# Moving token row factors, column sums and weight sums from TensorE and VectorE to memory and GpSimd in a one-core encoder layer

## The chip, the cores and the metric

The kernel runs on one core of one Trainium2 chip. The metric is the device time of one execution, in microseconds (us). The engines are named as in the profile: PE is TensorE, DVE is VectorE, ACT is ScalarE, POOL is GpSimd, SP is SyncE, which here issues all transfers.

## What is computed

One layer of a hybrid encoder on 4096 tokens of width 1024. The tokens are normalised, multiplied by one combined weight matrix, and split into attention operands (q, k, v), two gates (g_a, g_p) and a pooling branch u_p. Windowed attention and a multi-scale pooling are gated, concatenated, multiplied by an output matrix, normalised again and added to the input:

```
h = rmsnorm(x, pre_norm_g)
q, k, v, g_a, u_p, g_p = split(h @ w_in)
a = banded_attention(q, k, v, rel_bias, sink) * silu(g_a)
p = multiscale_pool(u_p, pool_w, pool_scale) * silu(g_p)
x = x + rmsnorm(concat(a, p) @ w_out, post_norm_g)
```

The input norm divides each token by the root of its mean square. That divisor is one number for each token, called the row factor below.

## The kernel before

**Two stages.** The first stage (up to about 495 us of the span) computes the three projections that need all channels of the pooling branch and the gates: GP (g_p), UU (u_p with the pooling matrices multiplied into its weights) and GA (g_a). The second stage does q, k, v, the attention and the output product, and is not touched.

**Numbers as pairs.** Every operand of a product is a pair of float16 tiles, high and low part, so that a product takes three matmuls. For token operands (tile `xb`, and `xt` for sums of token halves) ACT writes the high part and DVE then writes the low part as the difference (`b_low`, `t_low`, helper `tt`, L304). For weights (tile `wq`) ACT writes the high part (`w_high`, L557) and DVE the low part (`w_low`, helper `stt`, L307).

**Token groups.** The 4096 tokens are eight groups of 512, m = 0 to 7. Group 0 is multiplied plainly (`plain`, 192 matmuls for each of GP, UU, GA). Groups 1 to 7 use a Strassen-like scheme (`quad`) with seven products for each of the three projections; it needs sums of weight blocks S1 to S4 (`sum_weights`: four additions of 128x1024 float32 for each projection, then the pair for each sum) and sums of token blocks (`t_sums`: one addition of 512 and two of 256 columns). A product is issued in steps of six matmuls (one of four k blocks); in the profile the rows of L634 are these steps.

**Row factors.** For each group, ACT squares the token rows with a running sum, POOL takes the power -1/2 (`root`, tile `rs4`, one column for each 128 tokens), and PE spreads the 512 factors over all partitions by a product with the identity (`spread_all`, L413, four float32 matmuls that the profile shows as eight) into a PSUM tile `bc`. DVE then multiplies the group's token tile `nt` by gain and factor (`norm`, L307, eight instructions of 512 for a group) and makes the operands from it.

**Weight scales.** Before a weight becomes a pair it is scaled by a power of two from its largest column norm: ACT squares it into a bf16 tile `sq` (128x1024, `w_square`), PE adds the eight blocks of 128 columns and the partitions with eight matmuls against ones (`w_norm`, L528, tiles `n2ga`, `n2gb`, `n2a`, `n2u`, `n2b`), and DVE derives the scale (`w_scale`, from L188 on).

**What sets the order.** In the first stage each piece of work is a step with an engine, an estimated cost, a due time and its dependences (`do(...)`). A planner walks through these with the estimated costs, always taking the ready step with the lowest due time, and the instructions are then written out in that order. Each engine works its list strictly in order: an engine that comes to an instruction whose input isn't there waits, even if later ones could run. POOL's `tt` steps are costed with `pool(n)`, DVE's with `dve(n)`:

```
def dve(n):
    return 0.1 + n * 0.0012
def pool(n):
    return 0.15 + n * 0.0023
```

The planner knows nothing of one engine slowing another.

The helpers that record many operations have one line each: L304 is every two-tensor operation (`tt`), on DVE or POOL; L307 is every scalar-tensor-tensor on DVE (`stt`); L296 a tensor with a scalar.

Of the kernel before, what the change touches and what calls it, by code (L numbers as in the profile page):

```python
# [17 lines left out]
P = 128  # L18
S = 4096
D = 1024  # L20
KT = D // P
T = 512
NM = S // T
# [33 lines left out]
class Steps:  # L57
# [28 lines left out]
    def run(self):  # L86
        n_steps = len(self.steps)
        users = [[] for _ in range(n_steps)]
        open_deps = []
        for n, s in enumerate(self.steps):  # L90
            open_deps.append(len(s[5]))
            for d in s[5]:
                users[d].append(n)
        ready = [0.0] * n_steps
        begun = [None] * n_steps
        free = dict.fromkeys(("PE", "DVE", "ACT", "POOL", "SP"), 0.0)
# [38 lines left out]
def hybrid_layer(ctx: ExitStack, tc, io, out):  # L135
    nc = tc.nc
# [4 lines left out]
    dram = ctx.enter_context(tc.tile_pool(name="dram", bufs=1, space=DRAM))  # L141
# [8 lines left out]
    mhalf = const.tile([P, 1], F32, name="mhalf")  # L150
# [6 lines left out]
    sw = const.tile([P, 18], F32, name="sw")  # L157
# [5 lines left out]
    gs = const.tile([P, 1], F32, name="gs")  # L163
# [10 lines left out]
    epss = const.tile([P, 1], F32, name="epss")  # L174
    psc = const.tile([P, 4], F32, name="psc")

    f_row = dram.tile([NH, 512], F32, name="f_row")
    f_scr = dram.tile([NH, FR + 1, NF], F32, name="f_scr")
    x_scr = dram.tile([NU, P, 2, 2, HK, UT], F16, name="x_scr")
# [30 lines left out]
    with ExitStack() as actx:  # L210
        pa = actx.enter_context(tc.tile_pool(name="pa", bufs=1))
        psa = actx.enter_context(tc.tile_pool(name="psa", bufs=1, space=PSUM))

        GP, UU, GA = range(3)
# [6 lines left out]
        onesf = pa.tile([P, P], F32, name="onesf")  # L221
        edge = pa.tile([P, 4, 16], F32, name="edge")
        rs4 = pa.tile([P, 4], F32, name="rs4")
        xn1 = pa.tile([P, D], F32, name="xn")
# [4 lines left out]
        pw = ws[:, :T].rearrange("p (j c) -> p j c", j=4)  # L229
        turns = dict.fromkeys(("sq", "n2", "wup"), 0)  # L230

        def turn(name):
            turns[name] += 1
            return turns[name] % 2
# [68 lines left out]
        def tt(eng, out, in0, in1, op):  # L303
            eng.tensor_tensor(out=out, in0=in0, in1=in1, op=op)  # L304
# [210 lines left out]

        n2_t = {}

        def w_square(raw, z):
            A.activation(
                sqt[z].rearrange("p (g c) -> p g c", g=2) if len(raw.shape) == 3 else sqt[z], raw,  # L520
                AF.Square,
            )

        def w_norm(z, group, i, n, b):
            if i == 0:
                n2_t[group] = psa.tile([P, n, P], F32, name=f"n2{group}", tag=f"n2{b}")
            for k in range(KT):
                nc.tensor.matmul(  # L528
                    n2_t[group][:, i], ones16, sqt[z][:, k * P : (k + 1) * P], start=(k == 0),
                    stop=(k == KT - 1), skip_group_check=True,  # L530
                )

        def w_scale(group, cols):
# [4 lines left out]
        def w_gates(dst, cols):  # L538
            t_scalar(V, dst, isc[:, cols], 1.0 / H_SCALE, ALU.mult)

        def norms(keys, last, views, reads, group, cols):
            n, b = len(views), turn("n2")
            for i, (key, view, r) in enumerate(zip(keys, views, reads)):
                z = turn("sq")
                do("ACT", act(D), key, w_square, view, z, r=r, w=[f"sqt{z}"])
                do("PE", 0.5, key + 0.5, w_norm, z, group, i, n, b, r=["ones", f"sqt{z}"],
                   w=[f"n2{b}"])
# [29 lines left out]
        def sum_weights(q, scale, group, key, step, eng, again=False):  # L577
# [8 lines left out]
            if again:  # L586
# [11 lines left out]
            pair(q, S4, 1, scale, key + 3.5 * step, group)  # L598

        norms([5, 5], 5, [tile_view(GP, i) for i in (0, 1)], [tile_keys(GP, i) for i in (0, 1)],  # L600
              "ga", slice(0, 2))
        norms([13, 13], 13, [tile_view(GP, i) for i in (2, 3)], [tile_keys(GP, i) for i in (2, 3)],
              "gb", slice(2, 4))

        def gp_gates():
            w_gates(cg0, slice(0, 4))
# [67 lines left out]
                )  # L674


        cc = [pa.tile([P, 2, 2 * P], F32, name=f"cc{i}") for i in range(5)]
        cc_n = [0]

        def ccs(n):  # L680
# [219 lines left out]
        for j in range(4):  # L900
            ld(9.5 + 0.1 * j, wut[:, j], io["w_uT"][j], 0.5, w=[f"wut{j}"])
            z = turn("sq")
            for half in range(2):
                t = U0 + 4 * j + 2 * half
                do("PE", 1.0, t, u_prod, j, half, r=["ws", f"wut{j}"], w=[f"wup{half}"] + bcs)
                do("ACT", act(512), t + 1.2, u_square, j, half, z, r=[f"wup{half}"], w=[f"sqt{z}"])
                do("ACT", act(512), t + 1.2, u_keep, j, half, r=[f"wup{half}"],
                   w=[f"tile{UU}.{j}{half}"])
            do("PE", 0.5, U0 + 4 * j + 5, w_norm, z, "u4", j, 4, b, r=["ones", f"sqt{z}"],
               w=[f"n2{b}"])  # L910
# [16 lines left out]
        plain(GA, M0 + SL * 8 + 2)  # L927
        plain(UU, M0 + SL * 16 + 8)
        sum_weights(GP, com, "gc", M1 - 16, 3.0, "DVE", True)
        sum_weights(UU, sw[:, 8:9], "u4", M1 + 8, 3.0, "DVE")  # L930
        sum_weights(GA, sw[:, 4:5], "a4", M1 + 27, 3.0, "DVE")

        def prepare(m):
            key = start(m) - 55
            b = m % 2
            for i in range(4):
                xn, k = (xn1, "xn") if m > 1 or i % 2 == 0 else (NT[:, 2 * D : 3 * D], "ts")
                t = key - 9 + 3 * i if m > 1 else 20 + i
                ld(t - 3, xn, x_blk[BPM * m + i], 0.5, w=[k])
                do("ACT", 1.3, t, square, m, i, xn, w=[k, f"ssq{m % 2}.{i}"])  # L940
            do("POOL", 1.0, key + 3, root, m, slice(0, 4), r=[f"ssq{m % 2}.{i}" for i in range(4)] + ["mhalf"],
               w=["rs4", "rs0", "rs1"])
            do("PE", 1.2, key + 5, spread_all, m, r=["rs4", "ident"], w=[f"wup{m % 2}"])
            for c in range(HK):
                k = key + 14 + 9 * c
                n = f"n1.{c % 2}"
                ld(k - 9, n_view(m, c), xT[c][:, :, m], 0.5,
                   w=[n] + ([f"xsq{i}" for i in range(HK)] if m == 1 and c < 2 else []))
                for h in range(2):
                    do("DVE", dve(512), k + h, norm, m, c, h, r=["gs", f"wup{m % 2}"], w=[n])  # L950
# [1144 lines left out]
```

## Time and profile before

| | |
|---|---|
| median of 3 runs | 1174.7 us (1174.52 to 1175.09) |
| the profiled execution, its own time | 1174.91 us |
| its span, first to last instruction | 1172.8 us |
| PE busy | 1149.0 us, 98% of the span |
| PE weight loads busy | 883.4 us, 75% |
| DVE busy | 930.8 us, 79% |
| ACT busy | 702.6 us, 60% |
| POOL busy | 309.3 us, 26% |
| granted TensorE clock | 0.999 |

Rows of a timeline give the start in us from the span's beginning, the length of the merged piece in us, the engine, the line, the operation, output and inputs, and how many instructions are merged; a bracket at the end gives the idle time before it and what ended it. A PE row ends with the latency of its last matmul, which overlaps the next row, so the time that a piece takes from PE is the distance from its start to the next row's start. Rows of a source view give the least, median and greatest duration in ns.

### The profile page before, as it was taken

The page shows a single profiled execution, that of the slowest core. Times are in us where ns is not written, and L with a number is a line of the kernel's source. Part 1 is how long each engine was busy: PE and PEld are TensorE (multiplying, and loading weights), DVE is VectorE, ACT ScalarE, POOL GpSimd, SP SyncE. Part 2 cuts the span into 40 slices and gives each one's busy share as a digit, 9 for nine tenths or more (in the row PEclk, how much of TensorE's full clock was granted, in tenths as well). Part 3 has the DMA queues.
Part 4 walks back from the last instruction along what each step waited for, and adds up shares of the span by engine and source line. Part 5 has one row for each costly group of instructions (what it writes and reads, how often), then busy time and mean ns, then how long its engine had stood idle before and what let it go on. Part 6 is the DMA issues. An engine that isn't in the chain of part 4 may idle for free.

```text
span 1172.8 us, 33945 instructions
## 1 busy us (share of the span) xinstructions
PE 1149.0 (98%) x14304; PEld 883.4 (75%) x14304; DVE 930.8 (79%) x1865; ACT 702.6 (60%) x1459; POOL 309.3 (26%) x310
## 2 busy tenths in 40 slices
PE   5999999999999999999999999999999999999997
PEld 4998888888888888986667667576676667767653
DVE  6889997868788984558878878877887787887787
ACT  5875565546655552256676666666667666666672
POOL 0002111101101100201434434433533443443331
PEclk9999999999999999999999999999999999999999
DMA  8645488666756565299976886786777678687695
GB/s 315 218 111 169 162 261 268 185 234 221 255 189 232 153 186 176 56 279 209 263 184 140 191 198 133 197 196 159 182 193 185 142 190 200 136 194 160 164 234 144
DMA packets 292441, 224.65 MB, mean 192 GB/s; under 512 B 210704, under 2 KB 251920, under 8 KB 287680
## 3 DMA queue, kind: packets, MB, share of 16 engines
q1 hardware_dynamic: 292288, 222.48, 69.8%
q8 instruction: 112, 1.84, 0.6%
q14 instruction: 41, 0.34, 0.1%
HBM read 113.37 MB, written 60.33 MB: 148 GB/s over the span
## 4 chain that ended last, share of the span: by engine, by line
PE 50%; DVE 1%; ACT 0%; issue 0%; DVEq 0%; POOLq 0%; ACTq 0%
PE ms L1588 13%; PE aq L1227 12%; PE m L1588 9%; PE s L1272 4%; PE kv L1373 3%; PE o L1438 3%; PE kv L1227 3%; PE p L1438 2%; PE z L1560 1%; PE s L1560 0%; DVE pn L1336 0%; DVE mo L1627 0%; DVE p L1295 0%; ACT pn L1328 0%; DVE xt L1649 0%
## 5 line engine op out<-in xcount | busy, mean ns | idle before, releaser
L634 PEld LDWEIGHTS <-wq 128*128 128x128 f16 x4104 | 401.5, 98 | 52.7 <-issue 2.8
L634 PE MATMUL y<-xt,wq 128*128 128x256 f16 x1512 | 204.2, 273 | 0.9 <-ACT cc L742 0.9
L1306 ACT ACTIVATE p<-p,nm 128x385 f32<-128x385 f32 (+1 forms) x256 | 152.8, 599 | 35.0 <-POOL p L1289 20.3
L1227 PE MATMUL aq<-xb,xb 128*128 128x256 f16 x1024 | 173.4, 273 | 0.1
L1588 PE MATMUL ms<-wo,ys 128*128 128x512 f16 x720 | 162.7, 379 | 0.1
L1336 DVE SCALAR_TENSOR_TENSOR pn<-p,rd,pn 128x384 f16<-128x384 f32 (+1 forms) x256 | 156.1, 660 | 6.8 <-ACT pn L1328 6.8
L1295 DVE CUSTOM_DVE_ANT_0 p<-s,nt,nsink 128x384 f32<-128x384 f32 (+1 forms) x256 | 155.9, 665 | 1.8 <-PE s L1272 1.7
L1227 PEld LDWEIGHTS <-xb 128*128 128x128 f16 x1280 | 125.1, 98 | 22.8 <-issue 6.6
L1227 PE MATMUL aq<-xb,xt 128*128 128x256 f16 x512 | 139.6, 273 | 0.1
L1328 ACT ACTIVATE pn<-p,rd 128x384 f16<-128x384 f32 (+1 forms) x256 | 134.4, 596 | 4.2 <-issue 1.1
L1588 PEld LDWEIGHTS <-ys 128*128 128x128 f16 x720 | 69.2, 98 | 81.4 <-issue 2.8
L304 POOL TENSOR_TENSOR yt<-yt,sg 128x512 f32<-128x512 f32 (+2 forms) x32 | 48.0, 1499 | 311.4 <-DVE yt L307 293.1
L1588 PE MATMUL m<-wo,y 128*128 128x512 f16 x540 | 121.8, 379 | 0.0
L1588 PEld LDWEIGHTS <-y 128*128 128x128 f16 x540 | 51.5, 98 | 62.9 <-issue 2.9
L1622 POOL TENSOR_TENSOR mo<-mo,gpost 128x512 f32<-128x512 f32 x39 | 63.8, 1635 | 94.7 <-ACT jkb L1611 93.5
L634 PE MATMUL plain<-xb,wq 128*128 128x256 f16 x576 | 68.8, 276 | 3.0 <-ACT xb L446 1.8
L1227 PEld LDWEIGHTS <-xt 128*128 128x128 f16 x640 | 62.6, 98 | 8.3
L634 PE MATMUL y<-xb,wq 128*128 128x256 f16 x504 | 68.8, 273 | 0.0
L634 PE MATMUL v<-xb,wq 128*128 128x256 f16 x504 | 68.6, 273 | 0.2 <-DVE cc L304 0.2
L634 PE MATMUL v<-xt,wq 128*128 128x256 f16 x504 | 68.6, 273 | 0.0
L634 PE MATMUL x<-xb,wq 128*128 128x256 f16 x504 | 68.3, 273 | 0.0
L1272 PE MATMUL s<-k_all,q 64*32 64x288 f16 (+7 forms) x3648 | 62.5, 266 | 1.3 <-issue 1.3
(212 smaller groups left out, 1907.8 us busy)
## 6 DMA issues: line engine op xcount, KB each, us to landing
nt<-in_xT SPq DMA_DIRECT2D x28, 512.0 KB, 4.7
x_scr<-xb SPq DMA_DIRECT2D x14, 1024.0 KB, 7.2
xb<-x_scr SPq DMA_DIRECT2D x14, 1024.0 KB, 7.3
xr<-in_x SPq DMA_DIRECT2D x28, 512.0 KB, 4.6
out<-xr SPq DMA_DIRECT2D x28, 512.0 KB, 2.6
xn<-in_x SPq DMA_DIRECT2D x27, 512.0 KB, 4.4
ga_scr<-cc SPq DMA_DIRECT2D x64, 128.0 KB, 2.1
raw<-in_w_out SPq DMA_DIRECT2D x16, 512.0 KB, 5.4
```

Source lines behind the costliest of these rows:

```text
L304: eng.tensor_tensor(out=out, in0=in0, in1=in1, op=op)
L634: nc.tensor.matmul(b[:, s], wq[:, slot[q, op], wv, s, k, :], x[:, xv, k, :], start=(first and k + s + wv + xv == 0), stop=(last and k == H ...
L1227: nc.tensor.matmul(acc, w[:, j, k, :], x[:, kh, v, kt, :], start=(n == 0), stop=(n == 3 * KT - 1),)
L1272: nc.tensor.matmul(s_ps[qs, gg, c0:c1], q_t[u, half][a, qi, jj, tl + 32 * hq : tl + 32 * hq + 32], k_all[a, ki, kc + c0 - s0 : kc + c1 - s ...
L1295: nc.vector.tensor_tensor_reduce(out=p_t[b, half][:, hh, :nk], in0=s_t[jj][:, gg, :nk], in1=bias[:, h, lo : lo + nk], scale=negc[:, h : h ...
L1306: nc.scalar.activation(p[:, hh, : nk + 1], p[:, hh, : nk + 1], AF.Exp, bias=nm_t[b, half][:, hh : hh + 1], scale=-1.0, accum_out=den_t[b, ...
L1328: nc.scalar.activation(prob_view(b, half)[:, 0, i], p_t[b, half][:, i, :nk], AF.Copy, scale=rd_t[b, half][:, i : i + 1],)
L1336: nc.vector.scalar_tensor_tensor(out=pn4[:, 1, i], in0=p_t[b, half][:, i, :nk], scalar=rd_t[b, half][:, i : i + 1], in1=pn4[:, 0, i], op0= ...
L1373: nc.tensor.matmul(av[:, i], x[:, kh, v, kt, i * P : (i + 1) * P], w[:, B_V, k, :], start=(n == 0), stop=(n == 3 * KT - 1),)
L1438: nc.tensor.matmul(o_t[b][side][a, half], v_t[ku][ks, vi, kt, a], pt[b, half][ks, pi, g, :, kb - kbs[0], (LOW, TOP)[side]], start=start, s ...
L1588: nc.tensor.matmul(z_t[u, tag], y[:, k, yi, :], wo[o][:, wi, k, :], start=(n == 0 and acc is None), stop=(n == 3 * HK - 1), skip_group_che ...
L1622: eng.tensor_tensor(out=mo, in0=mo, in1=gpost[:, cs], op=ALU.mult)
```

## The change

**Row factors of groups 3 to 7.** `spread_all` on PE stays for groups 1 and 2. For the others POOL's `rs4` is written to a scratch in memory (`rows_store`, 512 single float32 elements), and read back as one row broadcast to 128 partitions (`rows_load`, 256 KB) into a new SBUF tile `rows`, which `norm` reads in place of the PSUM tile. The token squares and `root` of these groups get due times 16 us earlier. In the plan a made-up engine "NET" stands for 12 us and 7 us of transfer time; it issues nothing.

**Column sums folded.** For six of the weight squares (two of GA's four, three of UU's four, and the one of the v weights) POOL first adds the tile's eight blocks in three steps of 512, 256 and 128 columns (`w_fold`), and PE then needs one matmul in place of eight. GA's four squares get tiles of their own (the `cc` tiles, not yet in use then), in place of taking turns in two.

**Weight sums.** The four additions of UU and the four of GA move from DVE to POOL; GP's stay on DVE.

```diff
+        def rows_store(m):
+            nc.sync.dma_start(rs_scr[m].rearrange("(i p) -> p i", i=4), rs4)
+
+        def rows_load(m):
+            bc[m] = rows
+            nc.sync.dma_start(
+                rows, rs_scr[m].rearrange("(o t) -> o t", o=1).to_broadcast([P, T])
+            )
...
+        def w_fold(z):
+            for n in (512, 256, 128):
+                tt(G, sqt[z][:, :n], sqt[z][:, :n], sqt[z][:, n : 2 * n], ALU.add)
+
-        def w_norm(z, group, i, n, b):
+        def w_norm(z, group, i, n, b, folded):
...
-            for k in range(KT):
+            last = 1 if folded else KT
+            for k in range(last):
...
+        def norm_step(z, key, group, i, n, b, folded):
+            if folded:
+                do("POOL", 3.2, key, w_fold, z, w=[sq_key(z)])
+            do("PE", 0.1 if folded else 0.5, key, w_norm, z, group, i, n, b, folded,
+               r=["ones", sq_key(z)], w=[f"n2{b}"])
...
-                z = turn("sq")
+                z = turn("sq") if len(views) < 4 else 2 + i
...
+                norm_step(z, key + 0.5, group, i, n, b, folded and i < 2)
...
+            norm_step(z, U0 + 4 * j + 5, "u4", j, 4, b, j < 3)
...
-        sum_weights(UU, sw[:, 8:9], "u4", M1 + 8, 3.0, "DVE")
-        sum_weights(GA, sw[:, 4:5], "a4", M1 + 27, 3.0, "DVE")
+        sum_weights(UU, sw[:, 8:9], "u4", M1 + 8, 3.0, "POOL")
+        sum_weights(GA, sw[:, 4:5], "a4", M1 + 27, 3.0, "POOL")
+
+        MS = 3
...
-            do("PE", 1.2, key + 5, spread_all, m, r=["rs4", "ident"], w=[f"wup{m % 2}"])
+            if m < MS:
+                spread_key = f"wup{m % 2}"
+                do("PE", 1.2, key + 5, spread_all, m, r=["rs4", "ident"], w=[spread_key])
+            else:
+                spread_key = "rsp"
+                do("SP", 0.6, key - 12, rows_store, m, r=["rs4"], w=["rs_scr"])
+                do("NET", 12.0, key - 12, lambda: None, w=["rs_scr"])
+                do("SP", 0.45, key - 8, rows_load, m, r=["rs_scr"], w=["rsp"])
+                do("NET", 7.0, key - 8, lambda: None, w=["rsp"])
```

The changed costs make the planner write out a new order for the whole first stage. On PE the list has 89 rows fewer: five spreads, and 42 matmuls against ones with their weight loads. Three places matter below.

POOL, from its second `root` to the gates of the first token group, before (`rs` are row factors, `ssq` the sums of token squares, `yt` the gated pooling output):

```order
L296 TENSOR_SCALAR ssq_117<-ssq_117 128x2
L304 TENSOR_TENSOR rs_113<-ssq_117,mhalf 128x2
L296 TENSOR_SCALAR ssq_118<-ssq_118 128x4
L304 TENSOR_TENSOR rs_113<-ssq_118,mhalf 128x4
L304 TENSOR_TENSOR yt_119<-yt_119,sg 128x504
```

The same engine and stretch now, its middle part (`cc` and `sq` hold weight squares that are folded, `raw` is GA's weights, `wq` here UU's):

```order
L308 TENSOR_TENSOR cc_125<-cc_125 128x512
L308 TENSOR_TENSOR cc_125<-cc_125 128x256
L308 TENSOR_TENSOR cc_125<-cc_125 128x128
L308 TENSOR_TENSOR sq_118<-sq_118 128x512
L308 TENSOR_TENSOR sq_118<-sq_118 128x256
L308 TENSOR_TENSOR sq_118<-sq_118 128x128
L308 TENSOR_TENSOR raw<-raw 128x1024
L300 TENSOR_SCALAR ssq_120<-ssq_120 128x4
L308 TENSOR_TENSOR rs_114<-ssq_120,mhalf 128x4
...
L308 TENSOR_TENSOR raw<-raw 128x1024 x3
L308 TENSOR_TENSOR wq<-wq 128x1024 x4
L308 TENSOR_TENSOR yt_121<-yt_121,sg 128x504
```

Between these two rows of `root` and the first gate stood nothing on POOL; now fifteen folding additions and eight weight sums stand around the second of them.

DVE, while it makes the operands of token group 1, before (`nt` alone is a token sum, `nt<-nt,gsc,bc` a norm, `xb` and `xt` are low parts, `wq<-wq` a weight sum of UU, `wq<-wq,sw` the low part of a weight pair):

```order
L307 SCALAR_TENSOR_TENSOR wq<-wq,sw 128x1024 x2
L304 TENSOR_TENSOR nt<-nt 128x512
L304 TENSOR_TENSOR nt<-nt 128x256 x2
L304 TENSOR_TENSOR xb_68<-nt,xb_68 128x2x2x256
L304 TENSOR_TENSOR wq<-wq 128x1024
L304 TENSOR_TENSOR xt_105<-nt,xt_105 128x4x256
L307 SCALAR_TENSOR_TENSOR nt<-nt,gsc,bc_799 128x512
L304 TENSOR_TENSOR wq<-wq 128x1024
L307 SCALAR_TENSOR_TENSOR nt<-nt,gsc,bc_799 128x512
L304 TENSOR_TENSOR wq<-wq 128x1024
L304 TENSOR_TENSOR nt<-nt 128x512
```

The same place now, from the last pair of UU's plain weights on:

```order
L311 SCALAR_TENSOR_TENSOR wq<-wq,sw 128x1024 x2
L311 SCALAR_TENSOR_TENSOR nt<-nt,gsc,bc_791 128x512
L311 SCALAR_TENSOR_TENSOR wq<-raw,sw,wq 128x1024
L308 TENSOR_TENSOR nt<-nt 128x512
L308 TENSOR_TENSOR nt<-nt 128x256 x2
L308 TENSOR_TENSOR xb_68<-nt,xb_68 128x2x2x256
L311 SCALAR_TENSOR_TENSOR nt<-nt,gsc,bc_791 128x512
L308 TENSOR_TENSOR xt_106<-nt,xt_106 128x4x256
L311 SCALAR_TENSOR_TENSOR nt<-nt,gsc,bc_791 128x512
L311 SCALAR_TENSOR_TENSOR wq<-wq,sw 128x1024
L308 TENSOR_TENSOR nt<-nt 128x512
```

The three sums have gone from between the token work, and low parts of later weight sums have moved up into their place.

PE, at the first folded square of GA (`n2a` is the column norm, `wup` a product for UU's weights, `plain` a product of group 0):

```order
L908 MATMUL wup_0_455<-ws,xt_67 128x128 x4
L549 LDWEIGHTS ones_71
L549 MATMUL n2a_465<-cc_124,ones_71 128x128
L660 LDWEIGHTS wq
L660 MATMUL plain_447<-xb_66,wq 128x256
```

Here stood eight matmuls against ones; the one that is left comes 24 matmuls of group 0 and one `wup` product later in PE's list than the first of the eight did, and needs the fold on POOL.

More of the change, by code (lines that the diff above doesn't have):

```diff
@@ L95, in run @@
         begun = [None] * n_steps
-        free = dict.fromkeys(("PE", "DVE", "ACT", "POOL", "SP"), 0.0)
+        free = dict.fromkeys(("PE", "DVE", "ACT", "POOL", "SP", "NET"), 0.0)
         dma_free = 0.0
@@ L223, in hybrid_layer @@
         rs4 = pa.tile([P, 4], F32, name="rs4")
+        rows = pa.tile([P, T], F32, name="rows")
         xn1 = pa.tile([P, D], F32, name="xn")
@@ L229, in hybrid_layer @@
         pw = ws[:, :T].rearrange("p (j c) -> p j c", j=4)
+        cc = [pa.tile([P, 2, 2 * P], F32, name=f"cc{i}") for i in range(5)]
+        sqt += [t.rearrange("p s c -> p (s c)").bitcast(BF16) for t in cc[:4]]
         turns = dict.fromkeys(("sq", "n2", "wup"), 0)
@@ L516, in hybrid_layer, with sq_key @@
         n2_t = {}
+        def sq_key(z):
+            return f"sqt{z}" if z < 2 else f"cc{z - 2}"
         def w_square(raw, z):
@@ L539, in w_gates, with norms @@
             t_scalar(V, dst, isc[:, cols], 1.0 / H_SCALE, ALU.mult)
-        def norms(keys, last, views, reads, group, cols):
+        def norm_step(z, key, group, i, n, b, folded):
[3 more added lines that the diff above has]
+               r=["ones", sq_key(z)], w=[f"n2{b}"])
+        def norms(keys, last, views, reads, group, cols, folded=True):
             n, b = len(views), turn("n2")
             for i, (key, view, r) in enumerate(zip(keys, views, reads)):
-                z = turn("sq")
-                do("ACT", act(D), key, w_square, view, z, r=r, w=[f"sqt{z}"])
-                do("PE", 0.5, key + 0.5, w_norm, z, group, i, n, b, r=["ones", f"sqt{z}"],
-                   w=[f"n2{b}"])
+                z = turn("sq") if len(views) < 4 else 2 + i
+                do("ACT", act(D), key, w_square, view, z, r=r, w=[sq_key(z)])
+                norm_step(z, key + 0.5, group, i, n, b, folded and i < 2)
             do("DVE", 1.5, last, w_scale, group, cols, r=["gs"], w=[f"n2{b}", f"sw{group}"])
@@ L674, in ga_out @@
                 )
-        cc = [pa.tile([P, 2, 2 * P], F32, name=f"cc{i}") for i in range(5)]
         cc_n = [0]
@@ L937, in prepare @@
                 xn, k = (xn1, "xn") if m > 1 or i % 2 == 0 else (NT[:, 2 * D : 3 * D], "ts")
-                t = key - 9 + 3 * i if m > 1 else 20 + i
+                t = key - 9 - early + 3 * i if m > 1 else 20 + i
                 ld(t - 3, xn, x_blk[BPM * m + i], 0.5, w=[k])
                 do("ACT", 1.3, t, square, m, i, xn, w=[k, f"ssq{m % 2}.{i}"])
-            do("POOL", 1.0, key + 3, root, m, slice(0, 4), r=[f"ssq{m % 2}.{i}" for i in range(4)] + ["mhalf"],
+            do("POOL", 1.0, key + 3 - early, root, m, slice(0, 4), r=[f"ssq{m % 2}.{i}" for i in range(4)] + ["mhalf"],
                w=["rs4", "rs0", "rs1"])
-            do("PE", 1.2, key + 5, spread_all, m, r=["rs4", "ident"], w=[f"wup{m % 2}"])
+            if m < MS:
[7 more added lines that the diff above has]
+                do("NET", 7.0, key - 8, lambda: None, w=["rsp"])
             for c in range(HK):
@@ L949, in prepare @@
                 for h in range(2):
-                    do("DVE", dve(512), k + h, norm, m, c, h, r=["gs", f"wup{m % 2}"], w=[n])
+                    do("DVE", dve(512), k + h, norm, m, c, h, r=["gs", spread_key], w=[n])
                 x_operands(m, c, k + 2, "DVE")
```

12 lines of the change are left out of this document (6 added, 6 removed).

## The prediction

> **What bounds the kernel now.** I read the page first, then PE's waits, then the timelines of PE, DVE and POOL at the places where the order changes.
>
> ```profile
> span 1172.8 us, 33945 instructions
> PE 1149.0 (98%) x14304; PEld 883.4 (75%) x14304; DVE 930.8 (79%) x1865; ACT 702.6 (60%) x1459; POOL 309.3 (26%) x310
> ```
>
> PE is busy for all but 23.8 us of the span. PE's waits, longest first, say where the rest is:
>
> ```profile
> PE sp L370 <- DMA ident<-in_ident: 7.0, 1, 7.0
> ...
> PE y L634 <- ACT cc L742: 0.9, 1, 0.9
> ```
>
> The large one is the first load. In the rest of the first stage, after the start, PE waits 0.9 us at most at a time. So each us taken from PE's list is a us of the span, as long as its inputs still come in time; and each new wait of PE is a us lost. The prices of what is taken away are in PE's timeline at group 1's spread (start, us, instructions):
>
> ```profile
> 61.48 3.44 PE L634 MATMUL plain<-xb,wq 128*128 128x256 f16 x30
> 64.75 1.06 PE L413 MATMUL bc<-ident,rs 128*128 128x128 f32 x8
> 65.64 0.82 PE L634 MATMUL plain<-xb,wq 128*128 128x256 f16 x6
> 66.30 0.61 PE L528 MATMUL n2u<-sq,ones 128*128 128x128 bf16 x8
> 66.75 27.67 PE L634 MATMUL plain<-xb,wq 128*128 128x256 f16 x252
> ...
> 151.70 1.16 PE L413 MATMUL bc<-ident,rs 128*128 128x128 f32 x8 [0.33 <-POOL rs L304]
> ```
>
> From start to start, a spread takes 65.64 - 64.75 = 0.89 us, eight matmuls against ones 0.45 us or 0.056 each, a product matmul 3.27 / 30 = 0.109 us.
>
> **What the change takes from PE.** Five spreads: 5 x 0.89 = 4.45 us. The wait of 0.33 us in front of group 3's spread goes with it. Six foldings leave one matmul of eight: 42 x 0.056 = 2.35 us. Together 7.1 us. If nothing else happened, 1174.9 would become 1167.8 for the profiled execution; the median lies 0.2 below that execution, so 1167.6.
>
> **What it puts on POOL, and what that does to DVE.** The two engines are not independent. Timelines of DVE (first fence) and POOL (second), with one gate near 145 us and one near 102 us:
>
> ```profile
> 101.95 1.22 DVE L304 TENSOR_TENSOR xt<-nt,xt 128x1024 f16<-128x1024 f32 x1
> 103.09 2.27 DVE L307 SCALAR_TENSOR_TENSOR wq<-wq,sw 128x1024 f16<-128x1024 f32 x1
> ...
> 144.78 0.74 DVE L307 SCALAR_TENSOR_TENSOR nt<-nt,gsc,bc 128x512 f32<-128x512 f32 x1
> 145.44 1.39 DVE L304 TENSOR_TENSOR yt<-ubuf 128x527 f32<-128x527 f32 x1
> ```
>
> ```profile
> 102.11 2.16 POOL L304 TENSOR_TENSOR yt<-yt,sg 128x504 f32<-128x504 f32 x1 [2.60 <-DVE yt L307]
> ...
> 144.99 1.27 POOL L304 TENSOR_TENSOR yt<-yt,sg 128x512 f32<-128x512 f32 x1 [20.31 <-DVE yt L307]
> ```
>
> At 144.99 POOL starts a product of two SBUF tiles. The norm on DVE, whose second tensor is in PSUM, takes its usual 0.74. The next DVE operation reads two SBUF tiles and takes 1.39 in place of 0.70 (row at 99.67 below): it stands until POOL is done at about 146.2. At 102.11 it is POOL's turn to stand, until DVE's 1.22 us operation ends at 103.1; then POOL goes first, and DVE's next takes 2.27. So operations with two SBUF tensors shut each other out for their whole length, and take turns.
>
> How long are POOL's new operations? Rows by line, and by length for the smallest (busy, mean ns):
>
> ```profile
> L304 POOL TENSOR_TENSOR yt<-yt,sg x32: 1263/1280/2181, 96.2 to 496.2; 128x512 f32<-128x512 f32 x24, 128x504 f32<-128x504 f32 x4, 128x520 f32<-128x520 f32 x4
> L1494 POOL TENSOR_TENSOR y<-yf,y x30: 1152/1155/1281, 518.8 to 1119.3; 128x512 f16<-128x512 f32 x30
> L1289 POOL COPY p<-nsink 128x4 f32<-128x4 f32 x64 | 18.0, 296 | 0.1
> ```
>
> A weight sum has 1024 float32 columns: 2.25 us on the line through 4 and 512 columns, 2.55 at twice 512; I take 2.4. In a sentence of its own: the Trainium skill (GPSIMD Engine Reference, section 3.1) gives 4497 ns for 2048 float32 columns, an estimate of 2.25 us for 1024, by which the four sums below would hold DVE 0.6 us less in all. A fold in 16 bits: 1.15 + 0.72 + 0.51 (same line, 256 and 128 columns) = 2.4 us, between 2.0 (the halves at proportional cost) and 3.5 (three times the first).
>
> *At the start, 33 to 43 us.* ACT's squares, DVE's GP sums and low parts, PE:
>
> ```profile
> 31.68 2.00 ACT L519 ACTIVATE sq<-raw 128x1024 bf16<-128x1024 f32 x2
> ...
> ```
>
> ```profile
> 33.63 2.47 DVE L304 TENSOR_TENSOR wq<-wq 128x1024 f32<-128x1024 f32 x2
> 36.02 0.69 DVE L304 TENSOR_TENSOR xb<-xb,xb 128x512 f16<-128x512 f32 x1
> 36.62 2.48 DVE L304 TENSOR_TENSOR wq<-wq 128x1024 f32<-128x1024 f32 x2
> ...
> 40.87 0.72 DVE L296 TENSOR_SCALAR wq<-wq,rat 128x2048 f16<-128x2048 f16 x1
> ```
>
> ```profile
> 26.30 6.72 PE L634 MATMUL plain<-xb,wq 128*128 128x256 f16 x60
> ...
> 36.38 1.06 PE L883 MATMUL wup<-ws,xt 128*128 128x128 f32 x8
> 37.27 0.61 PE L528 MATMUL n2a<-sq,ones 128*128 128x128 bf16 x8
> ```
>
> The first square is there at 32.7. POOL's 512 columns run from 32.9 to 34.05, then DVE's first sum (1.2) to 35.25, POOL's 256 to 35.97, the second sum to 37.17, POOL's 128 to 37.7. In the new list 84 product matmuls and one `wup` (37.27 - 36.38 = 0.89) stand ahead of the single matmul: PE comes to it at 26.30 + 84 x 0.109 + 0.89 = 36.4 and waits 1.3. The second fold starts behind `xb` (0.60, 36.62 - 36.02) at 38.3 and, with a sum (1.2) and a rescale (0.65) between its steps, ends at 42.5; PE is there 30 matmuls after the first, 37.7 + 0.06 + 3.27 = 41.0, and waits 1.5. Each change of turn is about 0.13 cheaper than these additions (145.44 + 1.39 is 0.13 before 144.99 + 1.27 + 0.70); with that off at each of the ten changes the waits are 0.8 and 0.7. Between 2.8 and 1.5 I take 2.0; 0 if POOL is not held up between its steps, 3.5 if each fold costs its upper bound. The UU folds near 50 to 63 us fall where DVE waits for ACT, and PE reaches their matmuls 0.5 to 3 us after they end by the same reckoning: I take 0.
>
> *At group 1, 65 to 101 us.* This is the large term. DVE's work from the first norm to the last low part of `xb`, and PE's use of it:
>
> ```profile
> 65.84 1.41 DVE L307 SCALAR_TENSOR_TENSOR nt<-nt,gsc,bc 128x512 f32<-128x512 f32 x2 [3.02 <-PE bc L413]
> ...
> 70.30 1.60 DVE L304 TENSOR_TENSOR nt<-nt 128x512 f32<-128x512 f32 x3
> 71.82 2.48 DVE L307 SCALAR_TENSOR_TENSOR wq<-wq,sw 128x1024 f16<-128x1024 f32 x2
> 74.22 1.22 DVE L304 TENSOR_TENSOR xb<-nt,xb 128x1024 f16<-128x1024 f32 x1
> 76.49 2.48 DVE L307 SCALAR_TENSOR_TENSOR wq<-wq,sw 128x1024 f16<-128x1024 f32 x2
> ...
> 91.91 1.23 DVE L304 TENSOR_TENSOR xt<-nt,xt 128x1024 f16<-128x1024 f32 x1 [1.12 <-ACT xt L464]
> ...
> 94.52 0.71 DVE L304 TENSOR_TENSOR ws<-ubuf 128x527 f32<-128x527 f32 x1 [0.73 <-ACT ubuf L718]
> ...
> 96.07 2.54 DVE L304 TENSOR_TENSOR nt<-nt 128x512 f32<-128x512 f32 x3
> 98.53 1.22 DVE L304 TENSOR_TENSOR xb<-nt,xb 128x1024 f16<-128x1024 f32 x1
> 99.67 0.70 DVE L304 TENSOR_TENSOR yt<-ubuf 128x527 f32<-128x527 f32 x1
> ```
>
> ```profile
> 99.49 0.91 PE L634 MATMUL y<-xb,wq 128*128 128x256 f16 x6
> ```
>
> DVE has only 1.12 and 0.73 us idle in 34 us, and its low part ends at 98.53 + 1.22 = 99.75. PE's step that reads it starts at 99.49, reads the low part with its third matmul, and is 0.09 longer than the others: PE meets DVE with no margin at all.
>
> Now the same stretch in the new lists. The norm of group 1 starts 65.84 + 12 x 0.109 - 35 x 0.056 = 65.2 (12 product matmuls more, 35 against ones fewer ahead of it). To the end of the low part DVE needs 33.9 (65.84 to 99.75), less three UU sums (1.2 each, from 33.63 to 36.02), plus three low parts moved up (1.2 each, from 71.82 to 74.22), plus the second pooling step (101.95 - 99.67 = 2.3), plus that step's gate on POOL (2.54 against 1.60: 0.9), less the idle 1.85: 35.3, so 100.5. PE comes to the step with 24 product matmuls and group 2's spread more, 35 matmuls fewer ahead: 99.7 + 2.6 + 0.9 - 2.0 = 101.2. Without the weight sums, no wait.
>
> With them: UU's four start on POOL when the last low part of UU's plain weights is done, near 78.3 (76.49 + 2 x 1.2, less the 0.6 by which the norm starts earlier), in the middle of DVE's full stretch. Under the first a norm fits (0.66, 145.44 - 144.78), so DVE loses about 1.6; the next three stand each between two DVE operations on SBUF tiles (a low part and the three of `nt<-nt`) and cost 2.4 - 0.13 = 2.27 each. With 0.3 from the last of GA's sums, which mostly fall while DVE waits for the spread and the scale, that is 8.7. The low part ends at 109.2; PE waits 8.0. The start's 2.0 shifts both and drops out. Bounds: 5.5 (three norms fall under the sums) to 12 (2.55 each, two of GA's sums on full stretches too).
>
> **Sum.** -7.1 + 2.0 + 8.0 = +2.9: 1174.9 becomes 1177.8 for a profiled execution, 1177.6 as a median. Behind 101 us DVE has its three low parts and one more sum done, so I expect no further wait.
>
> **What I cost at nothing.** The rows from memory:
>
> ```profile
> yf<-yp_scr SPq DMA_DIRECT2D x32, 256.0 KB, 3.9
> yp_scr<-yt SPq DMA_DIRECT2D x28, 4.0 KB, 1.6
> ```
>
> Store and load at these prices take 5.5 us; the plan leaves 19 (the NET steps of 12 and 7 in the diff). A group's 21 products of 24 matmuls take PE 55 us, so group 3 starts near 205 us, some 50 us after its spread now, and that hides it. SP's list has stores and loads behind the `rows_store`, which waits for POOL's `root`: up to 2 us late each, with tiles loaded further ahead than that. `norm` then reads two SBUF tiles, 0.70 in place of 0.74 us at best, but waits for gates; no PE step depends on it that closely. If the cover is gone it costs its own delay, up to 3 us.
>
> **The rivals.** *1. PE's gain comes through* (faster). The turns on POOL do not lengthen DVE's stretch, because the sums fall elsewhere or POOL's operations slip into DVE's idle time. For it: POOL's eight sums are 19 us in a stretch of 45, and DVE sheds eight of its own. It decides below 0.7 us of loss on DVE; the break-even is 0.7 + 7.1 - 2.0 = 5.8 us. Price: -7.1 + 0 to 2: 1168 to 1170. Against it: the rows at 103.09 and 145.44. In a sentence of its own: the Trainium skill (SBUF — State Buffer, Who interferes with whom) says that a GpSimd read and a DVE instruction with two SBUF inputs shut each other out for the whole instruction, against this change, and the rows here agree (1.39 for 0.70). *2. Half of it* (about equal): norms under the sums, waits of 4 to 5 us: 1173 to 1175.5. *3. Memory as the wait* (slower): 512 single elements take far longer than the 4 KB row, SP stands at the load, and the loads behind it come late: +3 on the forecast or on rival 1. The Trainium skill (DMA: Bandwidth & Descriptors, Rules for kernel authors) says that a non-contiguous last dimension makes one descriptor for each element; no row here shows such a transfer's price.
>
> **How the numbers follow.** Forecast 0.50, with its own range 1174.5 to 1182; rival 1 0.30; rival 2 0.12; rival 3 0.08. About 0.2%, 2.35 us, is what a measurement can tell here. Slower by more (over 1177.05): 0.36 of the forecast and rival 3: 0.44. Within: 0.14 of the forecast and 0.07 of rival 2: 0.21. Faster: rival 1 and 0.05 of rival 2: 0.35. As both signs are likely, the range goes from rival 1's lower end to the forecast's upper: 1167.5 to 1181.5.
>
> **What would show it.** PE with a wait of some 8 us for DVE `xb` near 102 us, two of about 1 us each for POOL `cc` near 37 and 41, DVE operations of 3 us and more beside POOL's 1024 columns at 80 to 92 us. Wrong if DVE's low part of `xb` comes by 103 us, or if PE's waits after the start add up to under 5 us.

## The result and the profile after

The changed kernel takes 1185.6 us (1185.21 to 1186.48) against 1174.76 us: ratio 1.0093, 95% interval 1.0076 to 1.0111. It is slower by 10.8 us where the prediction said 2.9, and outside its range. The page of the changed kernel, its totals:

```profile
span 1183.8 us, 33808 instructions
PE 1146.2 (97%) x14222; PEld 876.6 (74%) x14222; DVE 941.0 (79%) x1857; ACT 702.8 (59%) x1459; POOL 355.6 (30%) x336
```

PE is busy for only 2.8 us less, although 7 us were taken from it. PE's waits (line, what it waited for, us in all, times, longest):

```profile
PE sp L374 <- DMA ident<-in_ident: 7.1, 1, 7.1
PE y L660 <- ACT ubuf L743: 4.6, 1, 4.6
PE n2ga L549 <- ACT sq L535: 4.0, 1, 4.0
PE y L660 <- ACT cc L767: 3.7, 3, 1.9
PE plain L660 <- DVE wq L311: 2.6, 3, 1.4
...
PE y L660 <- ACT sg L692: 1.6, 1, 1.6
...
PE n2a L549 <- POOL cc L308: 0.5, 1, 0.5
...
PE n2a L549 <- ACT cc L535: 0.5, 1, 0.5
```

The rows of 7.1 and 4.0 us lie at the start, where the kernel before has 7.0 and 3.6. Between 26 and 500 us PE's waits add up to 13.3 us, before the change to 1.4. The two of 0.5 are the folded squares at 37 and 41 us. The large one is at 98 us. Follow it back through four engines. POOL's timeline (start, us, instructions) has GA's last three sums (`raw`) and UU's four (`wq`):

```profile
63.78 8.09 POOL L308 TENSOR_TENSOR raw<-raw 128x1024 f32<-128x1024 f32 x3
82.31 10.88 POOL L308 TENSOR_TENSOR wq<-wq 128x1024 f32<-128x1024 f32 x4 [10.45 <-DVE wq L311]
```

DVE's timeline beside them:

```profile
45.31 0.17 DVE L209 TENSOR_SCALAR sw<-m 128x4 f32<-128x4 f32 x1
...
69.68 2.20 DVE L209 TENSOR_SCALAR sw<-m 128x4 f32<-128x4 f32 x1
...
82.81 2.94 DVE L311 SCALAR_TENSOR_TENSOR wq<-raw,sw,wq 128x1024 f16<-128x1024 f32 x1
85.67 7.80 DVE L308 TENSOR_TENSOR nt<-nt 128x512 f32<-128x512 f32 x3
...
100.84 1.28 DVE L311 SCALAR_TENSOR_TENSOR wq<-raw,sw,wq 128x1024 f16<-128x1024 f32 x1
...
111.39 1.22 DVE L308 TENSOR_TENSOR xb<-nt,xb 128x1024 f16<-128x1024 f32 x1
```

The three token additions take 7.80 where they took 1.60; the low part before them 2.94, and 1.28 when POOL is idle. (The first two rows are for later: a scale of four columns takes 0.17 us, and 2.20 beside GA's sums.) ACT's timeline:

```profile
93.51 1.04 ACT L477 CAST xt<-nt 128x1024 f16<-128x1024 f32 x1 [9.54 <-DVE nt L308]
94.47 0.68 ACT L743 ACTIVATE ubuf<-plain,uf 128x512 f32<-128x512 f32 x1
...
98.06 0.68 ACT L743 ACTIVATE ubuf<-plain,uf 128x512 f32<-128x512 f32 x1
99.82 1.04 ACT L477 CAST xt<-nt 128x1024 f16<-128x1024 f32 x1 [1.07 <-DVE nt L308]
...
101.82 0.67 ACT L743 ACTIVATE ubuf<-plain,uf 128x512 f32<-128x512 f32 x1
```

ACT stands 9.54 us at a cast of those sums (`xt<-nt`). Behind it in ACT's list are the evictions of UU's plain products (`ubuf<-plain`), whose data are long there: PE is done with the first three of these products by 94.8 us, and the third eviction starts at 101.82. PE needs the PSUM bank that the third of them frees:

```profile
97.16 0.82 PE L660 MATMUL plain<-xb,wq 128*128 128x256 f16 x6
102.54 1.44 PE L660 MATMUL y<-xb,wq 128*128 128x256 f16 x6 [4.56 <-ACT ubuf L743]
103.77 1.49 PE L660 MATMUL plain<-xb,wq 128*128 128x256 f16 x6
105.05 1.49 PE L660 MATMUL y<-xb,wq 128*128 128x256 f16 x6
106.33 1.42 PE L660 MATMUL plain<-xb,wq 128*128 128x256 f16 x6
107.58 0.82 PE L660 MATMUL y<-xb,wq 128*128 128x256 f16 x6
```

And the wait costs more than its 4.56 us: the four steps behind it start 1.23 to 1.28 us apart, not 0.65. The windows say why (stretch, its length, busy time and instructions of PE, PEld, DVE, ACT and POOL, and at the end the granted clock, the DMA share and GB/s):

```profile
98.00:102.50 4.50, 0.00 (x0) 0.00 (x0) 4.43 (x7) 3.43 (x6) 0.00 (x0) 0.80 0.52 134
102.50:107.50 5.00, 4.96 (x24) 3.44 (x24) 4.90 (x8) 3.11 (x4) 1.82 (x2) 0.50 0.88 274
107.50:112.00 4.50, 4.50 (x43) 4.10 (x42) 4.36 (x7) 1.60 (x3) 3.10 (x2) 1.00 0.36 112
```

After the wait PE ran at half clock for 5 us; that is 5.04 - 4 x 0.655 = 2.4 us more. The wait of 4.56 is worth 7.0.

### The profile page after: what moved, and what is told of

Its sections match the earlier page's. It is cut to its first block, busy times and chain, and to the rows that moved or that the text cites. A ratio compares the mean times of both kernels' runs of the same rounds, so it can differ in the third digit from the quotient of the medians.

```text
span 1183.8 us, 33808 instructions
## 1 busy us (share of the span) xinstructions
PE 1146.2 (97%) x14222; PEld 876.6 (74%) x14222; DVE 941.0 (79%) x1857; ACT 702.8 (59%) x1459; POOL 355.6 (30%) x336
## 5 line engine op out<-in xcount | busy, mean ns | idle before, releaser
L767 ACT COPY cc<-y 128x512 f32<-128x512 f32 x42 | 24.6, 585 | 75.5 <-PE y L660 71.3
```

Of the source, the lines that this page charges most:

```text
L767: A.copy(dst, bank_t[bk])
```

## The experiments

All times are medians of five rounds or more beside the kernel before on the same chip, whose medians in these rounds were 1174.4 to 1175.2. "+" and "-" in front of a time give the difference to that run's own before.

### Taking work out without moving an instruction

The planner goes by its estimated costs. An operation that is made short in the code keeps its place in every list, so these runs show the price of the operations apart from that of the order. The order is held, as it is called below.

`e1_sums_short`:

```
+                if eng == "POOL":
+                    o, x, y = o[:, :, :4], x[:, :, :4], y[:, :, :4]
                 do(eng, us, k, tt, e, o, x, y, op,
```

> The changed kernel in the same order, but GpSimd's eight weight sums work on 8 of their 1024 columns (the rest of the sums is left out). Theory 1, the sums on GpSimd shut VectorE out, ScalarE's evictions stand behind VectorE, and PE stands behind those: the wait of 4.6 us at 98 us, the half clock after it (2.4 us), the 1.4 us at 75 us and the 1.9 us at 127 us go, and 1185.6 becomes 1174 to 1177 us. Theory 2, the new order itself or the traffic of the row factors makes the waits: the time stays at 1183 us or more, with the wait near 98 us still above 3 us.

1173.4 us, ratio 0.9988 (0.9979 to 0.9996), -1.8: 12.6 us less than the changed kernel, and nothing of the waits at 75 and 98 us is left. Theory 1 holds (the time is 0.6 below its range), theory 2 falls. Of the 1.9 us near 127 us a wait of 1.05 is left, now at 118 us; and one of 2.2 us near 352 us, with half clock behind it.

`e16_uu_short`: the same with `and q == UU` in the condition.

> The changed kernel in its own order, with only UU's four weight sums on 8 columns (their rest is left out); GA's four keep their 1024 columns. If UU's sums are the loss: 1173.4 us of both short, plus the 1.4 us wait at 75 us that is GA's: 1175 us (1174 to 1176.5), and nothing of the 4.6 us near 98 us is left. Rival, GA's sums, which come first, make VectorE late: 1181 us or more.

1178.0 us, 1.0025 (1.0015 to 1.0035), +3.2; its runs scatter from 1174.7 to 1180.1. So UU's sums cost 10.8 - 3.2 = 7.6 us and GA's 3.2 + 1.8 = 5.0, the latter more than the 1.4 that I expected, by some 2 either way. The wait that is GA's own:

```profile
75.81 18.41 PE L662 MATMUL plain<-xb,wq 128*128 128x256 f16 x167 [1.42 <-DVE wq L311]
```

Its cause is the DVE row at 69.68 above: the scale of UU's weights, four columns, stands 2.2 us behind a sum of GA on POOL. In e1, with the same lists and the sums short, this operation takes 0.17 us. The other 3.6 us are small waits up to 231 us, of 0.7 to 1.8, that I didn't trace one by one.

`e13_short_16`: e1, and the row factors stored as 128 runs of 16 bytes (`"(p i) -> p i"` in `rows_store`). `e14_short_16_folds`: that, and the folds on 8 columns.

> The changed kernel in its order, with both suspects taken out: GpSimd's weight sums on 8 columns (the rest is left out), row factors stored in runs of 16 bytes (so they go to the wrong tokens of a group). Theory: 1173.4 us of the short sums less the wait of 2.2 us near 352 us and the half clock of 2 us behind it: 1169.3 us (1168 to 1171). Rival, a third cause is left: 1172 us or more.

> As the run before, and the folds work on 8 columns too, so that all of GpSimd's new work is gone and only what the change takes from PE is left. Theory: the waits of 0.5 us near 37 and 41 us go and the time comes down by 1 us, to 1168.3 us (1167 to 1170); the sum on paper of all that PE is spared is 1167.6. Rival, the folds' waits stay, since ScalarE's squares end them: no difference from the run before.

1170.76 us, 0.9969 (0.9957 to 0.9980), -3.9; and 1168.76 us, 0.9949 (0.9936 to 0.9963), -5.9. The stores cost 2.1 us in this order, the folds 2.0. What PE is spared is worth 5.9. The folds' 2.0 can be read from the two traces: e13 has the two waits of 0.5 us for folded squares and one of 1.04 at 118 us, and e14 has none of the three. The third lies behind the sixth fold, the one of the v weights, which POOL works on from 102.5 us in e13. A low part on DVE beside it and PE's later step:

```profile
103.65 2.18 DVE L308 TENSOR_TENSOR xt<-nt,xt 128x1024 f16<-128x1024 f32 x1
```

```profile
118.46 2.12 PE L662 MATMUL y<-xt,wq 128*128 128x256 f16 x18 [1.04 <-ACT cc L769]
```

In e14 this low part takes 1.22 us. ACT again has a cast of DVE's data ahead of the eviction for which PE waits, and stands 3.75 us at it in e13, 3.09 in e14. The first product of the output (m, first start) shows where the rest of the 7.1 is, before and in e14:

```profile
L1588 PE MATMUL m<-wo,y x540: 378/379/391, 529.4 to 1129.4; 128*128 128x512 f16 x180
```

```profile
L1625 PE MATMUL m<-wo,y x540: 379/379/390, 522.1 to 1123.1; 128*128 128x512 f16 x180
```

It comes 7.3 us earlier, but from there to the end of the span it takes 1167.7 - 522.1 = 645.6 us, before 1172.8 - 529.4 = 643.4. PE's instructions from the first attention output on are the same in the same order. In these two executions 1 us of it goes near 806 us, where e14 has a wait of 0.8 that the kernel before hasn't, and the rest behind 1120 us. Why this stage takes 2 us more isn't settled.

### The path near 100 us

`e5_filled_gap`, in `product`, once, ahead of the first y product:

```
+                    for _ in range(64):
+                        nc.tensor.matmul(fill[0][:, 0, :P], ones16, ones16, start=True,
+                                         stop=True, skip_group_check=True)
```

> The changed kernel with 64 added matmuls of 128 columns (some 3.6 us) on PE, into a spare PSUM bank, just ahead of the product that waits 4.6 us near 98 us; they run in that wait. Theory 1: the half clock of 2.4 us after the wait comes from PE standing idle, so the wait is filled, the clock stays at 1.0, and 1185.6 becomes 1183.2 us (1182.7 to 1184). Rival: the clock falls there for another reason, and the time stays at 1185.6 us or rises by up to 1 us.

1184.4 us, 1.0074 (1.0062 to 1.0086): between the two ranges given, and not told apart from 1185.6. Its trace shows why:

```profile
98.02 3.73 PE L673 MATMUL fill<-ones 128*128 128x128 bf16 x64 [0.82 <-ACT ubuf L751]
101.76 0.82 PE L661 MATMUL y<-xb,wq 128*128 128x256 f16 x6
102.41 0.82 PE L661 MATMUL plain<-xb,wq 128*128 128x256 f16 x6
...
113.19 0.70 PE L661 MATMUL y<-xb,wq 128*128 128x256 f16 x4 [2.24 <-DVE xb L308]
113.68 1.49 PE L661 MATMUL x<-xb,wq 128*128 128x256 f16 x6
```

The clock stayed up behind the filled gap (0.65 from step to step): standing idle is what halved it there. But PE then meets the low part of `xb` 2.24 us too early and loses the clock there. That is the wait that I predicted; in the changed kernel PE is late enough not to see it.

`e8_sums_alone`: the kernel before, with `"POOL"` for `"DVE"` in the two calls of `sum_weights` for UU and GA.

> The kernel before with only the eight weight sums moved to GpSimd. Theory 1, the sums lock VectorE in its full stretch wherever the planner puts them: 1180 to 1185 us, with a PE wait over 3 us between 75 and 125 us. Rival, they hurt only behind the folds, which keep GpSimd busy and push the sums into that stretch: 1173 to 1177 us.

1182.2 us, 1.0068 (1.0056 to 1.0081), +7.7. Theory 1. Without the folds and the stores PE meets both waits:

```profile
99.39 0.81 PE L634 MATMUL y<-xb,wq 128*128 128x256 f16 x6 [3.52 <-ACT ubuf L718]
107.64 0.88 PE L634 MATMUL y<-xb,wq 128*128 128x256 f16 x4 [2.63 <-DVE xb L304]
```

### The stores of single elements

`e17_stores_added`, in `prepare` of the kernel before; the lists of PE, DVE, ACT and POOL stay the same, row for row. `e18_stores_added_16` has `"(p i) -> p i"`.

```
+            if m >= 3:
+                do("SP", 0.0, key + 4,
+                   lambda: nc.sync.dma_start(rs_scr[m].rearrange("(i p) -> p i", i=4), rs4),
+                   r=["rs4"])
```

> The kernel before, every engine's order untouched, with five stores added on SP: the row factors of groups 3 to 7 go to memory as 512 single elements each and nobody reads them. Theory S (the stores hold up the transfers around them): PE waits of 3 to 8 us in all, 1177 to 1183 us. Rival, the stores hurt only together with the new order and its earlier loads: 1174.5 to 1175.5 us.

> As the run before, with the same bytes in 128 runs of 16 bytes. Theory S: no more than the kernel before, 1174.5 to 1175.5 us, and landing in 6 us or less. If any added transfer hurts, the same time as with single elements.

1179.8 us, 1.0047 (1.0035 to 1.0059), +5.0; and 1175.85 us, 1.0009 (1.0001 to 1.0018), +1.0. Theory S holds: five stores of 2 KB that nobody reads cost 5 us, as single elements. With 16-byte runs, which land in 2.7 to 8.9 us, the time is 0.35 above the range given for it. Windows behind the first store (issued at 153.3), e17 and then before (the last two numbers: DMA share, GB/s):

```profile
153.00:163.00 10.00, 10.00 (x98) 9.00 (x97) 9.74 (x14) 5.29 (x8) 1.27 (x1) 1.00 1.06 256
163.00:168.00 5.00, 5.00 (x48) 4.48 (x46) 4.90 (x10) 1.58 (x3) 1.27 (x1) 1.00 0.90 131
```

```profile
153.00:163.00 10.00, 10.00 (x98) 9.00 (x97) 9.74 (x13) 5.16 (x8) 1.27 (x1) 1.00 1.01 357
163.00:168.00 5.00, 5.00 (x49) 4.48 (x47) 4.90 (x10) 2.07 (x3) 1.28 (x1) 1.00 0.85 258
```

The transfer engines are about as busy as before and move a quarter to a half less. ACT and with it PE come late:

```profile
171.91 1.06 ACT L967 ACTIVATE sq<-raw 128x1024 bf16<-128x1024 f32 x1 [2.62 <-DMA raw<-in_w_b]
```

```profile
176.19 0.81 PE L635 MATMUL y<-xt,wq 128*128 128x256 f16 x6 [2.34 <-ACT cc L741]
```

`e9_rows_alone`: the change's row factors only, sums on DVE, no folds.

> Only the row factors of groups 3 to 7 go through memory; sums on VectorE, no folds. PE has 4.5 us less to do. Theory S: at least one PE wait over 1.5 us behind a store of single elements, 1172 to 1178 us. Rival, the route is hidden as forecast: 1170 to 1171 us, no new wait.

1187.3 us, 1.0108 (1.0089 to 1.0127), +12.9: far above theory S. DVE waits for the rows and PE for DVE, and the half clock comes twice:

```profile
174.56 2.74 DVE L311 SCALAR_TENSOR_TENSOR nt<-nt,gsc,rows 128x512 f32<-128x512 f32 x4 [5.00 <-DMA rows<-rs_scr]
```

```profile
179.54 0.81 PE L660 MATMUL x<-xb,wq 128*128 128x256 f16 x6 [3.39 <-DVE ubuf L311]
180.19 1.39 PE L660 MATMUL y<-xt,wq 128*128 128x256 f16 x6
181.37 1.48 PE L660 MATMUL x<-xb,wq 128*128 128x256 f16 x6
```

`e2_sums_back` has the sums of the change back on DVE (`"DVE"` in both calls); `e7_store_16_bytes` is e2 with `"(p i) -> p i"` in `rows_store`, so factors go to other tokens of the group.

> The changed kernel with the weight sums of both projections back on VectorE; row factors through memory and folded column sums stay. Theory 1 (the sums on GpSimd are the loss): 1171 to 1176 us, since PE keeps 7 us less to do and pays some 1 us at the start and up to 3 us where transfers come late. Theory 2 (order or memory route): 1181 us or more.

> The run before with the sums back on VectorE (1180.1 us), in the same order, but each row factor store writes 128 runs of 16 bytes in place of 512 single elements (so tokens within a group get each other's factors). Theory S, the single elements hold up all transfers issued around them, and the waits of 2.9 us near 290 us and 1.2 us near 345 us, with the half clock behind the first, come from that: 1174 us (1172 to 1176), stores landing in 3 us or less. Rival, those transfers are late because of the new order of loads: 1179 us or more, the waits stay.

1180.1 us, 1.0051 (1.0034 to 1.0068), between the two theories of e2, which is how the stores came under suspicion; and 1174.2 us, 0.9993 (0.9984 to 1.0001). In the same order the runs of 16 bytes are worth 5 us. Landing of the five stores, e2 and then e7 (3 us or less was expected of e7):

```profile
DMA to landing us min/median/max: 9.9/10.9/12.0
```

```profile
DMA to landing us min/median/max: 1.6/3.9/6.3
```

Two kernels try to keep the gain of this part. `e11_rows_alone_16` is e9 with 16-byte runs, and the norm reads them back in token order (`rows.rearrange("p (t i) -> p i t", i=4)`). `e15_rows_turned` is e9 with the tile turned by PE into 4 x 128, copied by ACT and stored as 4 runs of 512 bytes. `e12_store_16_in_all` is the whole change with e11's store and read.

> Only the row factors of groups 3 to 7 through memory, but stored as 128 runs of 16 bytes, and put back in token order by the norm, which reads them from SBUF with a stride of 16 bytes. Theory S (the single elements were the whole loss of that part): PE's 4.8 us come through, 1170 us (1169 to 1172), stores landing in 6 us or less, no PE wait over 1 us after 100 us, and the run beats both kernels. Rival, the earlier loads and the broadcast load crowd the transfers as well: 1174 us or more.

> The whole change, with the same store and read as the run before. Theory S: the waits of the changed kernel behind 180 us (0.5, 0.6, 1.3 and 1.6 us) go, and 1185.6 becomes 1181.7 us (1180.5 to 1183); the 4.6 us near 98 us stay. Rival, those waits come down from the lateness at 100 us: 1185 us or more.

> Only the row factors of groups 3 to 7 through memory, but PE turns the 128 x 4 tile into 4 x 128 first (one product of 128 float32 columns, 0.2 us a group in place of 0.9), ScalarE copies it, and the store writes 4 runs of 512 bytes; the norm reads a contiguous row tile again. PE has 3.4 us less to do than before, and the wait of 0.3 goes. Theory S with the strided read as the reason why the run with 16-byte runs gave 1175.8: 1171 us (1170 to 1172.5), faster than both kernels. Rival, the order with the early loads costs 3 us by itself: 1174 us or more.

e11: 1175.8 us, 1.0009 (1.0000 to 1.0017), 11.5 us below e9 but not faster than before. e15: 1176.9 us, 1.0017 (1.0008 to 1.0026). e12: 1182.9 us, 1.0075 (1.0062 to 1.0087), 2.7 below the change, inside its range but 1.2 above the middle of it. The strided read isn't free, by line, e11 and then e13, whose read is contiguous (us in all, mean ns):

```profile
L311 DVE SCALAR_TENSOR_TENSOR nt<-nt,gsc,rows 128x512 f32<-128x512 f32 x40 | 46.7, 1187 | 2.8 <-DMA rows<-rs_scr 2.5 <-DMA nt<-in_xT 0.3
```

```profile
L311 DVE SCALAR_TENSOR_TENSOR nt<-nt,gsc,rows 128x512 f32<-128x512 f32 x40 | 29.8, 771 | 2.8 <-DMA rows<-rs_scr 2.8
```

But e15 reads contiguous rows and is no faster, so the read alone isn't the reason. Between the 3.4 us that e15 spares PE and the 2.1 us that it is slower lie 5.5 us. Of these PE's waits in its trace show 3.0: in the first stage, after the start, 2.8 us in all against 1.4 before, behind it 4.0 against 2.4. Where the rest went stays open. No version with less on PE and the whole computation beat the kernel before.

### Single parts, planned anew

`e4_spreads_back`: `MS = NM`. `e10_folds_alone`: that and both sums on DVE. `e3_uu_back`: UU's sums on DVE.

> The changed kernel with all row factors spread by PE again; sums on GpSimd and folds stay. Theory 1: PE gets 4.5 us back to do and the late transfers near 345 us (2.9 us of PE waits) go, so 1186 to 1190 us, and the waits near 98 us stay. Theory 2b, the memory route is the loss: below 1181 us.

> Only the folds of column sums on GpSimd; sums on VectorE, all row factors on PE. PE has 2.4 us less to do and waits 1 us for folded squares near 37 and 41 us: 1173 to 1174 us if nothing else moves. Rival, the new order itself costs: the wait of 2.3 us near 125 us that the run with the sums back showed is here too, and the time is 1176 us or more.

> The changed kernel with UU's four weight sums back on VectorE, GA's four stay on GpSimd. If the loss is UU's sums in VectorE's full stretch, as the prediction has it: near the 1180.1 us of both back (1179 to 1182), and the wait of 1.4 us at 75 us stays, since it is GA's. Rival, GA's sums begin the lateness: 1184 us or more.

e4: 1183.7 us, 1.0075 (1.0062 to 1.0088): below the 1186 to 1190 of theory 1 and above the 1181 of its rival. PE has 4.5 us more to do and the time is 2 less, so without the memory route more is won than the route spared. But the order is a new one too, so this doesn't price the route by itself. e10: 1176.5 us, 1.0016 (1.0007 to 1.0025): the rival; the new order brings a wait of 2.34 us for DVE at 125 us, 60 us behind the fifth fold and before the sixth (139 us). e3: 1186.2 us, 1.0103 (1.0086 to 1.0121), which looks like its rival; but its trace has no wait between 76 and 120 us, and six of 1.0 to 2.8 us between 174 and 374, with the half clock twice. The one store whose landing its trace gives took 13.0 us. The new order had moved the loss, it seems to the transfers. So it tells nothing of GA and UU; e16 does.

## Why the prediction was wrong

The direction and the first cause were right, the sum was not. Three of its steps failed: GA's sums were taken to cost next to nothing, the stores nothing, and the wait that UU's sums make was put on the wrong path. In held order, each term beside what it measured:

| term | predicted | measured | from |
|---|---|---|---|
| taken from PE | -7.1 | -5.9 | e14 against before |
| folds (predicted: those at the start) | +2.0 | +2.0 | e13 and e14 |
| UU's sums | +8.0 | +7.6 | e16 and the change |
| GA's sums | 0.3, within UU's | +5.0 | e1 and e16 |
| stores | 0 | +2.1 | e1 and e13 |
| sum | +2.9 | +10.8 | |

The measured terms add up to 10.8 because each is the difference of two runs that follow each other, with one thing more taken out. So each holds for this sequence. A second sequence is on record for the sums together: with 16-byte stores in place first (e12, then e13) they are worth 12.2 us, here 7.6 + 5.0 = 12.6.

**What PE is spared**: 7.3 us at the end of the first stage, where 7.1 were added up; 2 us are lost again in the second.

**The folds**: the number is right by luck. The two waits at the start are 0.5 us each, where the 2.0 had about 1 each. The other 1.0 is the wait behind the fold of the v weights, for which the prediction has no term.

**UU's sums**: the lock-out was right in size (2.94 - 1.28 and 7.80 - 1.60 are 7.9 us on DVE; 8.4 were forecast). "PE waits 8.0" was not: the 7.6 are a wait of 4.6 and 2.4 of half clock, on another path. I followed DVE to the operand that PE reads, `xb`, and not to ACT. ACT's list has casts of DVE's sums ahead of PSUM evictions that need nothing from DVE, so a late DVE also keeps banks full. The low part came at 112.6 in place of 109.2 (the first norm starts 2.1 us later than reckoned, at 67.3, and the scale behind GA's sum costs 2.0 more), but PE was held up before it; e5 and e8 show that wait when the other is gone or shorter. Both waits come from the same lateness of DVE, and in the change PE reaches the step that reads the low part as this ends. So filling the first wait only uncovers the second (e5), and that 7.6 lies so close to 8.0 is in part chance.

**GA's sums**: the step that failed first. "Mostly fall while DVE waits for the spread and the scale" held for the time but not for its worth: DVE's little scale operation, on which UU's first weight pair depends, is itself shut out until POOL is done (2.20 us in place of about 0.2). That gives the wait of 1.4 at 75 us; how the other 3.6 come about stays open.

**The memory route**: the step "what I cost at nothing" failed. I priced the store by a row of 4 KB (1.6 us) and had the price of the single elements as unknown in a rival at 0.08, as a load that comes late. The damage is wider: around such a store, which takes 10 to 12 us to land in e2, the core's transfers move a quarter to a half less (e17). Loads of weights come late (ACT waits 2.62 us for one in e17), and so do stores of results that free a buffer (ACT waits 4.80 us for one in e2).

**The half clock** wasn't in the sum at all. It adds 2.4 us to a wait of 4.6.

## What to carry to other kernels

Before moving work to GpSimd, look for what VectorE does at that time with two SBUF tensors, and then follow VectorE's lateness to all who wait for it: the engine that evicts PSUM stands in one line, and an eviction behind a waiting cast holds TensorE as surely as a missing operand. Price a transfer by its number of runs, not by its bytes: here five stores of 512 runs of 4 bytes cost 5 us without a reader, and the same bytes in runs of 16 cost 1 us. And where an order is planned, take a cost out in place (a shorter operation in the same list) before undoing a part: here undoing one part moved the loss to another place twice (e10 and e3).

## What the hardware showed that I had not expected

- PE's clock fell to 0.50 behind idle stretches of 2.17 us (e1), 2.24 (e5), 2.63 (e8), 2.86 (e2), 3.39 (e9) and 4.56 us (the change), and stayed there for 3 to 5 us. It did not fall behind 2.34 (e10), 2.72 (e9, at 319 us) and 3.52 us (e8, at 99 us). So in these runs no length decides it alone. The Trainium skill (TensorE: Matmul & The Clock Gate, What's actually happening) has half clock after at least one idle window of about 3.4 us, in windows that run freely. The halving agrees; the length doesn't, since 2.2 us were enough at times.
- An operation with one SBUF input and four columns (`sw<-m`, 2.20 us in place of 0.17) stood behind POOL too; the rule of the prediction, two SBUF tensors, is too narrow. The Trainium skill (SBUF — State Buffer, Who interferes with whom) counts tensor_scalar among the operations that can take the shared port; this row fits.
- A DVE operation whose second tensor is read with a stride of 16 bytes took 1187 ns on average for 512 columns (e11), with a contiguous one 771 (e13).
